# The output projection's first product moved behind the m branch's second half, and the fifth product added to x by VectorE

## The chip, the cores and the metric

The kernel runs on one NeuronCore of one Trainium2 chip. The metric is the device time of one execution in microseconds (us); where several runs were made, the median stands for them. The profile is one execution of the same program, taken by the hardware profiler. TensorE is called PE in its lines, VectorE DVE, ScalarE ACT, GpSimd POOL and SyncE SP; a weight load of TensorE is PEld.

## The reference

The reference is a decoder trunk of two layers on 512 tokens of width 1024 in float32. Each layer has two branches beside each other, joins them, and adds a projection of the sum to `x`; then an MLP follows. The part that matters here is the joining and the output projection:

```
mixed = sigmoid(g_a) * (att @ w_att_branch) + sigmoid(g_m) * (hm @ w_m_branch)
x = x + mixed @ w_out
u = relu(rmsnorm(x, norm_ffn) @ w_ff1)
x = x + (u * u) @ w_ff2
```

`att` and `hm` are 512 x 512, `w_att_branch` and `w_m_branch` 512 x 1024, `w_out` 1024 x 1024. `hm` is the output of the mLSTM branch, here called the m branch.

## The kernel before

**Three matmuls for one.** Float32 operands are split into a high part (rounded to the PE's fast float32 format by an ACT copy) and a low part (what is left, by a DVE subtraction). A product of two split operands takes three PE matmuls (high x high, high x low, low x high), which `mm3` issues. A split (`split`, lines 172 to 181) is one ACT instruction and one DVE instruction that needs its result.

**The m branch's product in two halves.** `m_step(g, m, k)` makes the 512 x 1024 product `hm @ w_m_branch` in two column halves g = 0 and g = 1, with features along the partitions. A half has 16 steps (4 blocks m of 128 columns, 4 blocks k of 128 rows), 48 matmuls in all. When a block m is complete, `merge` reads its PSUM bank on DVE (line 950: gate times product; line 951: added to the attention branch's part in `wide[g]`, the tile `p` of the profile).

**The output projection in seven products.** `mixed @ w_out` is computed by a scheme with seven products in place of eight: tokens, inner columns and output columns are each cut in two, and sums of halves of the operands are multiplied. Each product has 8 steps (4 inner blocks k of 128, 2 token blocks i), 24 matmuls. `p_step(n, k, i)` makes product n. The token operand of each is in `u`, the weight operand in `wo[n, k]`.

- Product 1 multiplies `u[0, 0]`, the first token half of `wide[0]`, which needs only half g = 0 of the m branch.
- Product 5 multiplies `s1`, made by `sum1(p)` from `wide[1]` (line 986), which needs half g = 1. Products 6 and 3 multiply `s2` and `s4`, which `sum_next` makes in place from `s1` (line 992), one from the other. Product 7 multiplies `s3`, made by `sum3` (line 979) from `wide[0]` alone.
- The weight operands are sums of quadrants of `w_out`, built in the tiles `qa` and `qb` by DMAs that add in flight and that POOL issues (`sum_a`, line 1016, and line 1055); each sum may start only when the split of the one before has read the tile. They are split by `ready_w` and `ready_pair`.

**Where results go.** Product 1 fills two PSUM banks called "x", product 5 two called "y", product 2 two called "f". Products 6, 7 and 4 add onto "x", product 3 onto "y". So each product's state of a bank has to be read before the next product writes to it. The table `outs` says how it is read: `onto` lets DVE add (or subtract) the bank to a quarter of `x` (line 1088); `onto_later` lets ACT copy the bank, with its sign, to a staging tile `st` (line 1094), and POOL then adds that to `x` by a DMA (line 1095). The staging tiles are two, taken by i, and share one place for all who stage.

**What sets the order.** The list `fill` gives the steps of PE one after another, each 0.25 wide; the list `side` gives the preparing work (splits, sums, loads, with their places in the same measure), and `weave` merges the two. A scheduler then orders each engine's instructions, with those under `tc.high_priority()` placed ahead. Engines run their own lists in order and wait for each other by semaphores. The places of `side` don't depend on which step of `fill` stands at that place.

Of the kernel before, what the change touches and what calls it, by code (L numbers as in the profile page):

```python
# [33 lines left out]
def hybrid_kernel(ctx, tc, x, norm_mix, w_in, att_q_norm, att_k_norm, att_sinks, m_gate_bias,  # L34
# [50 lines left out]
    def bank():  # L85
        return now["psum"].tile([P, T], F32, tag="m", name=nm("mm"), bufs=5)
# [43 lines left out]
    def g_ffn(l, k):  # L130
        return gcol[:, 16 + 8 * l + k:17 + 8 * l + k]
# [51 lines left out]
    def mm3(ps, sh, sl, mh, ml, first, last, **kw):  # L183
        one = pe.matmul(ps, sh, mh, start=first, stop=False, **kw)
        pe.matmul(ps, sh, ml, start=False, stop=False, **kw)
        pe.matmul(ps, sl, mh, start=False, stop=last, **kw)
        return one
# [201 lines left out]
    def mixer(l, norm, late, order, phase):  # L389
# [303 lines left out]
        def gate_steps(g, last=False):  # L693


            sg = []

            def ev(m, ps):
                sg.append(wide[g][:, m, :] if g < 2 else slot())
                ve.tensor_tensor(sg[m], ps, row[0], op=ALU.mult)  # L700
                if m == 3:
                    for t in sg:
                        i = sc.activation(t, t, AF.Tanh, scale=0.5)  # L703
                    if last:
                        with tc.issue_after(i.ins):
                            sc.preload_act_table_set(LN_EXP)

            return sg, feat_steps(acts, wcols(C_G + 512 * g, 512), ev)
# [147 lines left out]
        g1, s1 = gate_steps(1)  # L856
# [91 lines left out]
        def merge(g, m, ps):  # L948
            t = wide[g][:, m, :]
            ve.scalar_tensor_tensor(sgm[g][m], sgm[g][m], 1.0, ps, op0=ALU.add, op1=ALU.mult)  # L950
            ve.tensor_tensor(t, t, sgm[g][m], op=ALU.add)  # L951
# [16 lines left out]
        def direct(t, g, p):  # L968
            with behind():
                u[t, g, p] = split(part(t, g, p), get=pair)  # L970
# [12 lines left out]
        def sum1(p):  # L983
            if p == 0:
                scratch["b"] = mid.tile([P, 4, H], F32, tag="mid6", name=nm("sc"))
            ve.tensor_tensor(scratch["b"][:, 2 * p:2 * p + 2, :], part(1, 1, p), part(1, 0, p), op=ALU.subtract)
            of_chain("s1", p)
# [79 lines left out]
        def m_step(g, m, k):  # L1067
            if k == 0:
                now_m[g, m] = bank()
            ps, c = now_m[g, m], slice(m * P, (m + 1) * P)  # L1070
            mm3(ps, *(w[:, c] for w in wm[g, k]), *hmT[k], k == 0, k == 3)
            if k == 3:
                with tc.high_priority():
                    merge(g, m, ps)
                    if m % 2:
                        if g:
                            sum1(m // 2)
                        else:
                            direct(0, 0, m // 2)

        now_m = {}
        m_order = [(m, k) for m2, ks in (((0, 1), (0, 1)), ((0, 1), (2, 3))) for m in m2 for k in ks]
# [7 lines left out]
        def onto_later(t, j, i, ps):  # L1090

            with tc.high_priority():
# [1 line left out]
                sc.activation(stage, ps, AF.Copy, scale=-1.0 if j else 1.0)  # L1094
                gp.dma_start(xtok[t][j][:, i, :], stage, accum_op=ALU.add)

        outs = {1: ("x", (0, 0), [(onto_later, 0, 0)]), 5: ("y", "s1", [(onto_later, 1, 1)]),
                6: ("x", "s2", [(onto, 0, 1)]), 3: ("y", "s4", [(onto, 0, 1)]), 7: ("x", "s3", [(onto, 1, 1)]),
                2: ("f", (0, 1), [(onto, 0, 0)]), 4: ("x", (1, 1), [(onto, 1, 0)])}

        def p_step(n, k, i):
            which, key, ends = outs[n]
            fresh = n in (1, 5, 2) and k == 0
            if fresh and i == 0:
                held[which] = [bank(), bank()]
            ah, al = (a[:, k % 2, i * P:(i + 1) * P]
                      for a in u[(*key, k // 2) if isinstance(key, tuple) else (key, k // 2)])
            mm3(held[which][i], ah, al, *wo[n, k], fresh, False, skip_group_check=True)
            if k == 3:
                for f, t, j in ends:  # L1110
                    f(t, j, i, held[which][i])

        def p_steps(n, order_=by_weights):
            return [(0.25, lambda k=k, i=i: p_step(n, k, i)) for k, i in order_]

        norm = Norm(lambda k: g_ffn(l, k))
        fill = [(0.25, lambda m=m, k=k: m_step(0, m, k)) for m, k in m_order] + p_steps(1)
        fill += [(0.25, lambda m=m, k=k: m_step(1, m, k)) for m, k in m_order]
        for n in (5, 6, 3, 7, 2):
            fill += p_steps(n)  # L1120
        fill += p_steps(4, by_tokens)
        side = [(0.3, lambda: ready_w(1, 3)), (2.3, lambda: ready_pair(5, 0)), (4.3, lambda: ready_pair(5, 1)),
# [507 lines left out]
    for l in range(DEPTH):  # L1630
        with start if l == 0 else ExitStack() as phase:
            if l > 0:
                psum_pools(phase, 3)
            norm = mixer(l, norm, late, order, phase)
        late = norm.steps(0, 1.5, 0.5)
        with ExitStack() as phase:
            psum_pools(phase, 2)
            norm = mlp(l, norm, late, phase)
        late = norm.steps(0, 1.5, 0.5, lambda k, norm=norm: turn_behind(norm, k)) if norm else []
        order = [4, 5, 6, 7, 0, 1, 2, 3]  # L1640
# [40 lines left out]
```

## Time and profile before

| | |
|---|---|
| Median of 3 runs | 1286.1 us (1283.01 to 1287.47) |
| The profiled execution's own time | 1284.8 us |
| Its span, first to last instruction | 1283.1 us |
| PE busy | 1267.5 us (99%) |
| PE weight loads busy | 1088.1 us (85%) |
| DVE busy | 1038.5 us (81%) |
| ACT busy | 795.6 us (62%) |
| POOL busy | 260.6 us (20%) |
| Granted PE clock | 1.0 in every slice |

The span is 1.7 us below the execution's own time, and that is 1.3 us below the median of the runs. PE is busy nearly all the time, so what can be gained without taking matmuls away is in the few places where PE waits. The output projection of layer 0 runs from about 260 us to 325 us, that of layer 1 from about 895 us to 960 us. Between and behind them lie the MLPs and the second layer's mixer.

### The profile page before, as it was taken

What the parts mean: (1) busy time and instruction counts of PE and PEld (TensorE: products, weight loads), DVE (VectorE), ACT (ScalarE), POOL (GpSimd) and SP (SyncE); (2) the same over time, 40 slices, a digit from 0 to 9 for tenths busy, and PEclk for the clock granted to TensorE, in tenths of its full rate; (3) what the DMA queues carried; (4) which work ended last, traced back from release to release, by engine and by line L of the source; (5) the groups of instructions that cost most, each with busy time, mean ns of one, the idle gap of its engine ahead of it and who ended that gap; (6) DMA issues with size and microseconds to landing.
All of it is one profiled execution on the core that took longest, in us unless ns stands there. A gap on an engine that the chain in (4) does not pass through costs nothing.

```text
span 1283.1 us, 19225 instructions
## 1 busy us (share of the span) xinstructions
PE 1267.5 (99%) x6882; PEld 1088.1 (85%) x6882; DVE 1038.5 (81%) x1650; ACT 795.6 (62%) x1403; POOL 260.6 (20%) x341
## 2 busy tenths in 40 slices
PE   8999999999999999999999999999999999999998
PEld 6877888887889999999888778888788899999987
DVE  4689988678687897968957889876787879789697
ACT  5478579645665665656554875785465656565563
POOL 4413132021003021131114031310310120301210
PEclk9999999999999999999999999999999999999999
DMA  5426372576669888898224254634856697988953
GB/s 157 111 59 158 106 131 77 154 138 144 186 164 193 234 182 211 195 207 216 34 75 116 63 151 107 115 109 138 164 139 182 164 220 192 201 213 193 212 149 99
DMA packets 139503, 194.39 MB, mean 152 GB/s; under 512 B 10632, under 2 KB 79088, under 8 KB 139408
## 3 DMA queue, kind: packets, MB, share of 16 engines
q1 hardware_dynamic: 92992, 129.72, 33.0%
q0 software_dynamic: 45696, 63.05, 30.7%
q8 instruction: 54, 0.88, 0.3%
q10 hardware_dynamic: 720, 0.40, 0.1%
q14 instruction: 41, 0.34, 0.1%
HBM read 188.95 MB, written 2.10 MB: 149 GB/s over the span
## 4 chain that ended last, share of the span: by engine, by line
PE 86%; DVE 5%; ACT 5%; DMA 2%; issue 1%; DVEq 0%; SPq 0%; ACTq 0%
PE mm L47 70%; PE aux L47 15%; PE aux L52 2%; DMA qa<-in_w_out_dram 1%; ACT t L618 1%; DVE wl L167 1%; DVE p L951 1%; DVE a L950 1%; DMA w<-in_w_in_dram 1%; ACT wh L1162 0%; ACT wh L166 0%; DVE t L653 0%; DVE a L700 0%; ACT t L585 0%; ACT p L703 0%
## 5 line engine op out<-in xcount | busy, mean ns | idle before, releaser
L47 PE MATMUL mm<-i,wh 128*128 128x512 f32 (+1 forms) x1280 | 353.8, 363 | 0.3
L1162 ACT ACTIVATE wh<-raw 128x1024 fp32r<-128x1024 f32 x212 | 223.2, 1056 | 177.6 <-PE mm L47 94.3
L1163 DVE TENSOR_TENSOR wl<-raw,wh 128x1024 fp32r<-128x1024 f32 x212 | 255.6, 1221 | 80.4 <-ACT wh L1162 80.3
L47 PEld LDWEIGHTS mm<-i,wh 128*128 128x128 f32 x1280 | 223.0, 189 | 31.3 <-ACT wh L1162 0.7
L47 PE MATMUL mm<-i,wl 128*128 128x512 f32 (+1 forms) x640 | 229.1, 358 | 0.0
L47 PE MATMUL mm<-wh,uh 128*128 128x512 f32 x440 | 171.8, 390 | 0.0
L47 PE MATMUL mm<-wl,uh 128*128 128x512 f32 x440 | 171.7, 390 | 0.0
L47 PE MATMUL mm<-wh,ul 128*128 128x512 f32 x440 | 171.2, 389 | 0.0
L1332 POOL DMA_DIRECT2D raw<-in_w_ff_dram x48 | 62.5, 1309 | 383.1 <-DMA raw<-in_w_ff_dram 212.9
L47 PEld LDWEIGHTS mm<-i,wl 128*128 128x128 f32 x640 | 120.9, 189 | 18.1
L167 DVE TENSOR_TENSOR wl<-w,wh 128x512 fp32r<-128x512 f32 (+1 forms) x144 | 97.4, 678 | 46.2 <-ACT wh L166 45.1
L166 ACT ACTIVATE wh<-w 128x512 fp32r<-128x512 f32 (+1 forms) x144 | 86.4, 604 | 71.1 <-PE mm L47 49.4
L47 PE MATMUL mm<-wh,i 128*128 128x512 f32 (+1 forms) x352 | 100.6, 359 | 2.2 <-ACT i L179 1.5
L1217 DVE SCALAR_TENSOR_TENSOR x<-mm,ms,x 128x512 f32<-128x512 f32 x126 | 90.6, 744 | 8.5 <-PE mm L47 8.5
L47 PEld LDWEIGHTS mm<-wh,ul 128*128 128x128 f32 x440 | 82.6, 188 | 17.4
L47 PEld LDWEIGHTS mm<-wh,uh 128*128 128x128 f32 x440 | 82.8, 188 | 16.1
L47 PEld LDWEIGHTS mm<-wl,uh 128*128 128x128 f32 x440 | 82.8, 188 | 15.5
L1489 POOL DMA_DIRECT2D raw<-in_w_ff_dram x36 | 43.3, 1204 | 148.4 <-DVE wl L1163 106.1
L47 PEld LDWEIGHTS mm<-wh,i 128*128 128x128 f32 x352 | 62.0, 188 | 12.1 <-ACT i L179 1.9
L47 PE MATMUL aux<-i,wh 128*128 128x256 f32 x384 | 69.6, 283 | 0.0
L47 PE MATMUL aux<-t,wh 128*128 128x256 f32 x384 | 69.6, 283 | 0.0
L47 PE MATMUL mm<-wl,i 128*128 128x512 f32 (+1 forms) x176 | 61.9, 352 | 0.0
(317 smaller groups left out, 2522.0 us busy)
## 6 DMA issues: line engine op xcount, KB each, us to landing
raw<-in_w_ff_dram SPq DMA_DIRECT2D x144, 512.0 KB, 5.1
raw<-in_w_ff_dram POOLq DMA_DIRECT2D x84, 512.0 KB, 7.9
w<-in_w_in_dram SPq DMA_DIRECT2D x112, 256.0 KB, 2.7
a<-in_w_in_dram POOLq DMA_DIRECT2D x32, 256.0 KB, 6.1
qa<-in_w_out_dram POOLq DMA_DIRECT2D x12, 512.0 KB, 6.3
a<-in_w_in_dram SPq DMA_DIRECT2D x16, 256.0 KB, 4.3
w<-in_w_att_branch_dram SPq DMA_DIRECT2D x16, 256.0 KB, 2.9
w<-in_w_m_branch_dram SPq DMA_DIRECT2D x16, 256.0 KB, 2.9
```

Of the source, the lines that this page charges most:

```text
L47: latest[0] = nc.tensor.matmul(*args, **kw)
L52: latest[0] = nc.tensor.transpose(*args)
L166: sc.activation(wh[:, :off], raw[:, :off], AF.Copy)
L167: ve.tensor_tensor(wl[:, :off], raw[:, :off], f32(wh[:, :off]), op=ALU.subtract)
L618: sc.activation(s3[:, i, :], s3[:, i, :], AF.Exp, bias=m[:, i:i + 1], accum_out=den[:, i:i + 1])
L950: ve.scalar_tensor_tensor(sgm[g][m], sgm[g][m], 1.0, ps, op0=ALU.add, op1=ALU.mult)
L951: ve.tensor_tensor(t, t, sgm[g][m], op=ALU.add)
L1162: sc.activation(hi, src, AF.Copy)
L1163: ve.tensor_tensor(lo, src, f32(hi), op=ALU.subtract)
L1217: ve.scalar_tensor_tensor(xh[:, cc], ps[i][:, cc], ms[j][:, b:b + 1], xh[:, cc], op0=ALU.mult, op1=ALU.add)
L1332: gp.dma_start(to[h], src(h, i, j), accum_op=ALU.add)
L1489: gp.dma_start(to[h], src(h, i, j), accum_op=ALU.add)
```

## The change

Product 1 is moved, and the results of product 5 take the other way to `x`. In `fill`, the 8 steps of product 1 stood between the two halves of the m branch's product; now the halves follow each other, and product 1 comes behind the second, ahead of product 5. The places in `side` stay as they are. In `outs`, product 5 gets `onto` in place of `onto_later`. The sign is the same.

```
-        outs = {1: ("x", (0, 0), [(onto_later, 0, 0)]), 5: ("y", "s1", [(onto_later, 1, 1)]),
+        outs = {1: ("x", (0, 0), [(onto_later, 0, 0)]), 5: ("y", "s1", [(onto, 1, 1)]),
...
-        fill = [(0.25, lambda m=m, k=k: m_step(0, m, k)) for m, k in m_order] + p_steps(1)
-        fill += [(0.25, lambda m=m, k=k: m_step(1, m, k)) for m, k in m_order]
-        for n in (5, 6, 3, 7, 2):
+        fill = [(0.25, lambda m=m, k=k: m_step(0, m, k)) for m, k in m_order] + [
+            (0.25, lambda m=m, k=k: m_step(1, m, k)) for m, k in m_order]
+        for n in (1, 5, 6, 3, 7, 2):
```

Both layers get it, since both are built by the same function. What it moves is shown for layer 0; layer 1 moves alike. The rows are the instructions in an engine's order: line, operation, output <- inputs, and the output's size.

On PE, before, at the end of the first half (bank mm_3192 holds its last block m = 3) product 1 follows, into bank mm_3211, with weights wh and wl as first operand:

```order
L47 MATMUL mm_3192<-a_3115,t_2882 128x512
L47 MATMUL mm_3192<-a_3116,t_2882 128x512
L47 MATMUL mm_3192<-a_3115,t_2883 128x512
L47 MATMUL mm_3211<-wh_3040,a_3168 128x512
L47 MATMUL mm_3211<-wl_3041,a_3168 128x512
L47 MATMUL mm_3211<-wh_3040,a_3169 128x512
```

At the same place after the change the second half's first block stands (a_3036 and a_3037 are the split `hm`, a_2691 and a_2692 split weights of the m branch):

```order
L47 MATMUL mm_3192<-a_3115,t_2882 128x512
L47 MATMUL mm_3192<-a_3116,t_2882 128x512
L47 MATMUL mm_3192<-a_3115,t_2883 128x512
L47 MATMUL mm_3211<-a_3036,a_2691 128x512
L47 MATMUL mm_3211<-a_3037,a_2691 128x512
L47 MATMUL mm_3211<-a_3036,a_2692 128x512
```

The 24 matmuls of product 1 now stand behind the 48 of the second half; the 24 of product 5 follow them, and from there PE's list goes on with the same products as before.

On ACT, before, from the splits of `s3` (sc_3234) on. The rows `st` are product 1's two copies (taken from mm_3211 and mm_3212; they stand first) and product 5's; sc_3304 is the tile of s1, s2 and s4, i_3268 the high parts of product 6's weights, t_3291 and t_3335 those of product 3's:

```order
L1094 ACTIVATE st_3261<-mm_3212 128x512
L176 ACTIVATE a_3236<-sc_3234 128x512
L176 ACTIVATE a_3240<-sc_3234 128x512
L176 ACTIVATE i_3268<-qa_2974 128x1024
L176 ACTIVATE t_3291<-t_3222 128x512
L176 ACTIVATE a_3306<-sc_3304 128x512
L176 ACTIVATE i_3268<-qa_2974 128x1024
L176 ACTIVATE t_3335<-t_3227 128x512
L176 ACTIVATE a_3349<-sc_3304 128x512
L176 ACTIVATE a_3366<-sc_3304 128x512
L1094 ACTIVATE st_3403<-mm_3355 128x512
L1094 ACTIVATE st_3418<-mm_3356 128x512
```

After the change, the same stretch (sc_3262 is the tile of s1, s2 and s4; i_3272, t_3295 and t_3336 are the weights; mm_3313 and mm_3314 are product 1's banks):

```order
L176 ACTIVATE a_3236<-sc_3234 128x512
L176 ACTIVATE a_3240<-sc_3234 128x512
L176 ACTIVATE a_3264<-sc_3262 128x512
L176 ACTIVATE i_3272<-qa_2974 128x1024
L176 ACTIVATE t_3295<-t_3221 128x512
L176 ACTIVATE a_3309<-sc_3262 128x512
L176 ACTIVATE i_3272<-qa_2974 128x1024
L1094 ACTIVATE st_3344<-mm_3313 128x512
L1094 ACTIVATE st_3350<-mm_3314 128x512
L176 ACTIVATE t_3336<-t_3227 128x512
L176 ACTIVATE a_3366<-sc_3262 128x512
L176 ACTIVATE a_3370<-sc_3262 128x512
```

Product 1's two copies moved behind the splits of s1 (a_3264 and a_3309), the split of s1's first part moved ahead of product 6's weights, and product 5's copies are gone.

On DVE, before, around the second part of s1 (a_3350 is its low part; a_3125 is the last merge of the second half; the L992 rows turn s1 into s2 and s2 into s4):

```order
L177 TENSOR_TENSOR i_3269<-qa_2974,i_3268 128x1024
L950 SCALAR_TENSOR_TENSOR a_3125<-a_3125,mm_3328 128x512
L177 TENSOR_TENSOR t_3336<-t_3227,t_3335 128x512
L951 TENSOR_TENSOR p_643<-p_643,a_3125 128x512
L986 TENSOR_TENSOR sc_3304<-p_643,p_642 128x512
L177 TENSOR_TENSOR a_3350<-sc_3304,a_3349 128x512
L992 SCALAR_TENSOR_TENSOR sc_3304<-sc_3304,p_642 128x1024
L177 TENSOR_TENSOR a_3367<-sc_3304,a_3366 128x512
L177 TENSOR_TENSOR a_3371<-sc_3304,a_3370 128x512
L177 TENSOR_TENSOR t_3380<-t_3232,t_3379 128x512
L177 TENSOR_TENSOR t_3393<-t_3247,t_3392 128x512
L992 SCALAR_TENSOR_TENSOR sc_3304<-sc_3304,p_643 128x1024
```

After the change, from the second part of s1 on (a_3310 is its low part; mm_3355 and mm_3356 are product 5's banks, x_1_90 the quarter of `x` that it belongs to):

```order
L986 TENSOR_TENSOR sc_3262<-p_643,p_642 128x512
L177 TENSOR_TENSOR t_3296<-t_3221,t_3295 128x512
L177 TENSOR_TENSOR a_3310<-sc_3262,a_3309 128x512
L177 TENSOR_TENSOR i_3273<-qa_2974,i_3272 128x1024
L177 TENSOR_TENSOR t_3337<-t_3227,t_3336 128x512
L992 SCALAR_TENSOR_TENSOR sc_3262<-sc_3262,p_642 128x1024
L177 TENSOR_TENSOR a_3367<-sc_3262,a_3366 128x512
L177 TENSOR_TENSOR a_3371<-sc_3262,a_3370 128x512
L1088 TENSOR_TENSOR x_1_90<-x_1_90,mm_3355 128x512
L1088 TENSOR_TENSOR x_1_90<-x_1_90,mm_3356 128x512
L177 TENSOR_TENSOR t_3380<-t_3232,t_3379 128x512
L177 TENSOR_TENSOR t_3393<-t_3247,t_3392 128x512
```

Product 5's two subtractions now stand between the splits of s2 and product 3's last weights. POOL has two DMAs fewer in each layer, and product 1's two adding DMAs moved behind later weight sums in POOL's list. SP's list keeps its order.

## Prediction

> **What bounds the kernel now.** I read the page's busy shares first, then who PE waits for in the whole run, then PE's timeline over the output projection of each layer, then the chain that led to the wait found there.
>
> ```profile
> PE 1267.5 (99%) x6882; PEld 1088.1 (85%) x6882; DVE 1038.5 (81%) x1650; ACT 795.6 (62%) x1403; POOL 260.6 (20%) x341
> PE mm L47 <- ACT a L176: 3.7, 2, 2.1
> ...
> PE aux L52 <- ACT wh L166: 0.3, 2, 0.2
> ```
>
> PE is the bound. Its longest named wait in the run (us in total, times, longest) is 3.7 us in two places, on a split (line 176): one per layer, both in product 5. The list has nine rows, of which the first and the last stand here; none names lines 1162 or 1163, which split the MLP's weights. PE's timeline (start, duration, instructions, [idle before <- releaser]), layer 0 and then layer 1:
>
> ```profile
> 271.43 0.39 PE L47 MATMUL mm<-wh,a 128*128 128x512 f32 x1
> ...
> 276.89 0.84 PE L47 MATMUL mm<-a,a 128*128 128x512 f32 x3
> ...
> 287.77 2.88 PE L47 MATMUL mm<-i,a 128*128 128x512 f32 x12
> 292.26 8.48 PE L47 MATMUL mm<-i,a 128*128 128x512 f32 x36 [1.61 <-ACT a L176]
> 300.58 5.67 PE L47 MATMUL mm<-t,a 128*128 128x512 f32 x24
> 306.09 0.39 PE L47 MATMUL mm<-wh,a 128*128 128x512 f32 x1
> ```
> ```profile
> 922.38 2.88 PE L47 MATMUL mm<-i,a 128*128 128x512 f32 x12
> 927.40 8.53 PE L47 MATMUL mm<-i,a 128*128 128x512 f32 x36 [2.13 <-ACT a L176]
> 935.76 5.74 PE L47 MATMUL mm<-t,a 128*128 128x512 f32 x24
> 941.34 0.39 PE L47 MATMUL mm<-wh,a 128*128 128x512 f32 x1
> ```
>
> Product 1 starts at 271.43, the second half of the m branch at 276.89, product 5 at 287.77 with 12 matmuls, then PE stands until 292.26; 6 and 3 follow, and product 7 starts at 306.09. The chain of waits says why:
>
> ```profile
> 288.94 0.68 DVE a L950
> 289.62 0.60 DVE t L177
> 290.22 0.61 DVE p L951
> 290.85 0.70 DVE sc L986
> 291.56 0.02 issue
> 291.58 0.64 ACT a L176
> 292.22 0.04 issue
> 292.26 22.16 PE mm L47 x96
> ```
>
> The second part of s1 needs the last merge of the second half, whose matmuls end just before product 5. Only product 5's own first 12 matmuls cover merge, subtraction and split, and DVE comes to the merge 1 us late.
>
> **What the stall is worth.** The second half's 48 matmuls take 287.77 - 276.89 = 10.88 us, 0.2267 us each, so 24 take 5.44 us. From the start of product 5 to that of product 7 are 72 matmuls, 16.32 us. It took 306.09 - 287.77 = 18.32 us in layer 0 and 941.34 - 922.38 = 18.96 us in layer 1: 2.00 and 2.64 us lost, 4.64 together. The idle that is printed is 1.61 + 2.13 = 3.74 us; the rest is the restart and the shorter waits of products 6 and 3 on the same DVE.
>
> **The move of product 1.** It puts 5.44 us of matmuls between the last merge and product 5. I replayed DVE's and ACT's new lists by hand in layer 0's times, with these durations:
>
> ```profile
> L177 DVE TENSOR_TENSOR i<-qa,i 128x1024 fp32r<-128x1024 f32 x3 | 3.7, 1224 | 1.4 <-ACT i L176 1.4
> L951 DVE TENSOR_TENSOR p<-p,a 128x512 f32<-128x512 f32 x6 | 4.1, 688 | 0.1
> L1088 DVE TENSOR_TENSOR x<-x,mm 128x512 f32<-128x512 f32 x2 | 1.4, 682 | 0.6 <-PE mm L47 0.6
> L992 DVE SCALAR_TENSOR_TENSOR sc<-sc,p 128x1024 f32<-128x1024 f32 x2 | 2.4, 1222 | 0.0
> 271.63 0.69 DVE L950 SCALAR_TENSOR_TENSOR a<-a,mm 128x512 f32<-128x512 f32 x1 [0.22 <-PE mm L47]
> ...
> 273.74 0.69 DVE L177 TENSOR_TENSOR a<-p,a 128x512 fp32r<-128x512 f32 x1 [0.70 <-ACT a L176]
> 274.69 1.23 DVE L177 TENSOR_TENSOR i<-qa,i 128x1024 fp32r<-128x1024 f32 x1 [0.26 <-ACT i L176]
> 275.83 1.22 DVE L979 TENSOR_TENSOR sc<-p 128x1024 f32<-128x1024 f32 x1
> 278.24 1.29 DVE L177 TENSOR_TENSOR a<-sc,a 128x512 fp32r<-128x512 f32 x2 [1.18 <-ACT a L176]
> 280.69 1.23 DVE L177 TENSOR_TENSOR i<-qa,i 128x1024 fp32r<-128x1024 f32 x1 [1.16 <-ACT i L176]
> ```
>
> On DVE 128x1024 operations follow each other at 1.14 us (274.69 to 275.83), 128x512 ones at 0.60, or 0.70 where one needs the result of the one before (289.62 to 290.22, 290.85 to 291.56 above); a split's ACT part takes 0.64. The first half ends as before, so the second runs 271.43 to 282.31, product 1 to 287.75, product 5 to 293.2, product 6 to 298.6, product 3 to 304.1, if nothing waits.
>
> - DVE is free at 275.83 and takes the merges as blocks finish (275.7, 277.1, 279.8, 282.5, with 0.2 for the last matmul's way, as in the row at 271.63), with s3 between them. The last merge starts at 282.5; behind it stand a_3265, the add, product 6's first weights (1.14) and then s1's second part, ready at 286.1; ACT's split ends at 286.8, DVE's at 287.5. Product 5 needs them at 287.75 + 2.72 = 290.5: 3.0 us to spare. The first part is ready at 283.7, due at 287.75.
> - s2: i_3273 to 288.9, t_3337 to 290.0 (it waits for ACT, which copies product 1's banks from 287.7 to 288.8), line 992 to 291.2, first split 291.9 and 292.5. Product 6 needs the high part at 293.2 and the low part two matmuls later, 293.65: 1.1 us to spare.
> - s4: the two subtractions of product 5 to 294.3, two weights to 295.5, line 992 to 296.7, split 297.4 and 298.1; due at 298.6 and 299.1: 1.0 us. Its second split follows two adds of product 6, at 300.1, due at 301.8.
>
> So no wait is left up to product 7 in the replay. Bounds: at least the printed 3.74 us if the short waits stay, at most 4.64. I take 4.6, as every margin is 1 us or more, above the shorts' size. Nothing else of PE moves; product 1's operands exist since 274.4 (the row at 273.74), and the five banks in rotation are read by DVE well before they are taken again.
>
> **Product 5's way to x.** Removed per layer: two ACT copies, two adding DMAs; added: two DVE subtractions.
>
> ```profile
> L1094 ACT ACTIVATE st<-mm x8: 580/598/601, 276.4 to 930.5; 128x512 f32<-128x512 f32 x8
> DMA to landing us min/median/max: 3.3/5.5/8.6
> ...
> DMA to landing us min/median/max: 4.5/6.5/8.3
> ...
> 323.93 1.28 DVE L1088 TENSOR_TENSOR x<-x,mm 128x512 f32<-128x512 f32 x2
> ```
>
> The landing times are those of line 1095 (to x) and of line 1055 (product 7's weight sums). ACT gains 2 x 0.60 us and waits anyway: zero. DVE pays 2 x 0.60, inside the 5.44 us of product 6; in the s4 sum above, cost zero on PE. Were that cover gone, 1.2 us a layer. DVE now waits for PE at these two, and t_3380, t_3393, s4 and its splits are queued behind. Product 1's two copies sit in front of s2's split on ACT, but that one waits for DVE until 291.2: zero. They are also done (288.8) before product 6 adds onto the same banks (293.2).
>
> The pages were read against this too. "Perfetto Trace Analysis" of the Trainium skill, section "Optimizing Scalar/DVE Operations", gives VectorE about 125 ns of access overhead on PSUM against 60 on SBUF, and ACT 51 against 93, which speaks for leaving the bank to ACT; by that the four subtractions would cost 4 x 0.065 = 0.26 us more of DVE. The trace doesn't show it: 682 ns with a PSUM input, 688 without.
>
> **Queues.** POOL: product 1's second adding DMA now stands behind a weight sum that needs i_3273 (288.9) and one that needs t_3337 (290.0), so it is issued at about 291 in place of 278 and lands by 300 with the longest landing shown (8.6). That quarter of x is next read by product 2's add, in the row at 323.93: hidden. The first three of product 7's weight sums are issued up to 12 us ahead of it, the last at 296.7; with 8.3 us to land it is there at 305, needed at 307. SP keeps its order; its loads of product 2's weights wait for PE's use of m branch tiles, which ends 5.5 us earlier, and the MLP's second load waits for product 1's staging, free before product 5's was: earlier, worth nothing to PE.
>
> **What comes behind.** PE's waits name no line of the MLP's weights, so layer 0's gain should pass through the MLP into layer 1.
>
> **Rivals.**
>
> 1. The stall moves to product 6 or 3. For: the same DVE work stays due, and margins are 1.0 to 1.1 us; against: DVE had waits to fill between 271 and 281 (0.70, 0.26, 1.18, 1.16 us in the rows above). If DVE is 3.3 us later than replayed, each layer pays 2.2 us again: 4.6 - 4.4 = 0.2 us gained, 1285.9; 2.2 us later gives 4.6 - 2.2 = 2.4, 1283.7.
>
> 2. Slower, by a late weight sum. DMA is full where the chain needs the second part of product 6's weights:
>
> ```profile
> 278.00:285.00 7.00, 7.00 (x32) 5.81 (x31) 5.54 (x8) 2.30 (x4) 3.39 (x4) 1.00 1.01 163
> 276.21 1.21 POOL L1016 DMA_DIRECT2D qa<-in_w_out_dram  x1 [3.91 <-DVE i L177]
> 286.46 1.04 ACT L176 ACTIVATE i<-qa 128x1024 fp32r<-128x1024 f32 x1
> 287.02 0.53 SPq L1189 DMA_DIRECT2D raw<-in_w_ff_dram  x1
> DMA to landing us min/median/max: 5.7/6.3/9.0
> ```
>
> The stretch's DMA share (second last column) is 1.01. The MLP's first 512 KB load now goes at about 282.5, when s3's split has freed its place, in place of 287.0. ACT reaches this weight at 286.7, in order, and s2 stands behind it. The landing times are those of line 1016. From landing to s2's first split 5.3 us pass (1.05 + 1.2 + 0.6 on ACT, 0.6 + 1.2 on DVE, 0.64 on ACT), so it must land by 287.9; the longest landing, 9.0 from 277.4, is 286.4. It decides beyond 287.9 + 2.3 = 290.2, 12.8 us after issue; at 15 us each layer pays 4.5 us, 9.0 - 4.6 = 4.4 us slower, 1290.5. Against it: product 1's 2 x 256 KB leave that stretch. "DMA: Bandwidth & Descriptors" of the Trainium skill, section "Anatomy of one DMA — SWDGE (gpsimd) path", fits 2.0 us + bytes / 436e3 to such a DMA, by which 512 KB would take an estimated 3.2 us and never be late. The rows, 5.7 to 9.0 us, are above it, and the rival goes by them.
>
> 3. One layer's gain is lost behind the projection, because loads pace the MLP: 1286.1 - 2.64 = 1283.5. For: PE's idle is only named, not the slack behind it; against: the absent waits.
>
> **How the numbers follow.** From its own 1284.8 us the execution comes to 1280.2; the median of the runs stands 1.3 us above it, so I forecast 1286.1 - 4.6 = 1281.5 us. A measurement of this kernel tells about 0.3%, 3.9 us. Chances: forecast 0.62, rival 1 0.18, rival 3 0.10, rival 2 0.10. The forecast is a gain of 0.29% to 0.36%, so 0.06 of it counts as within 0.3%, with rivals 1 and 3: faster 0.56, same 0.34, slower 0.10. Range: 1279.2 (4.64 us from the median and half the runs' spread, 2.2) to 1286.0 (rival 1); rival 2 and some of each tail are left out.
>
> **What would show it.** Right: PE's wait on line 176 in product 5 gone in both layers; 16.3 us from product 5's start to product 7's; the m branch's 96 matmuls without a gap; ACT's `st` rows four, at about 288 and 920 (634.6 us later, less layer 0's gain). Wrong: a PE wait at product 6 or 3 on a split of line 176 or 177 (rivals 1, 2; with ACT waiting for `qa` before it, rival 2), or first waits of PE inside an MLP (rival 3).

## The result and the profile after

The changed kernel takes 1278.74 us, the median of 6 runs (1278.26 to 1278.96). The kernel before took 1283.04 us beside it (6 runs, 1282.71 to 1287.47). The medians lie 4.3 us apart. The ratio is 0.9962, with a 95% interval of 0.9951 to 0.9972: faster by 0.38% (4.9 us by this ratio), a little more than the 0.3% that a measurement can tell from no change. In a later comparison it was 1278.54 against 1283.29 us, 4.75 us apart, ratio 0.9962 (0.9948 to 0.9976). The forecast of 1281.5 us is 2.8 us too high, and the time lies 0.46 us below the low end of its range.

The profiled execution took 1278.87 us, with a span of 1277.2 us. Its page's busy shares:

```profile
PE 1267.0 (99%) x6882; PEld 1089.3 (85%) x6882; DVE 1040.0 (81%) x1654; ACT 793.5 (62%) x1399; POOL 257.0 (20%) x337
```

From the list of PE's waits in the whole run (us in total, times, longest), the first and the last of seven rows:

```profile
PE aux L52 <- DVE t L653: 1.8, 4, 0.5
...
PE aux L47 <- ACT t L585: 0.2, 1, 0.2
```

The row that led this list before, 3.7 us on a split of line 176, is gone. PE's timeline over the same place, layer 0 and then layer 1:

```profile
287.35 11.04 PE L47 MATMUL mm<-i,a 128*128 128x512 f32 x48
298.23 5.60 PE L47 MATMUL mm<-t,a 128*128 128x512 f32 x24
303.67 0.39 PE L47 MATMUL mm<-wh,a 128*128 128x512 f32 x1
...
919.56 11.04 PE L47 MATMUL mm<-i,a 128*128 128x512 f32 x48
930.44 5.60 PE L47 MATMUL mm<-t,a 128*128 128x512 f32 x24
935.88 0.39 PE L47 MATMUL mm<-wh,a 128*128 128x512 f32 x1
```

Products 5 and 6 are one row of 48 matmuls without idle time, and product 3 follows. From product 5's start to product 7's are 303.67 - 287.35 = 16.32 us, and 935.88 - 919.56 = 16.32 us: PE's own time for 72 matmuls, to the hundredth. Before, it was 18.32 and 18.96 us.

DVE's timeline in layer 0, from the second part of s1 to the split of s4:

```profile
285.05 0.68 DVE L986 TENSOR_TENSOR sc<-p,p 128x512 f32<-128x512 f32 x1
...
289.49 1.22 DVE L992 SCALAR_TENSOR_TENSOR sc<-sc,p 128x1024 f32<-128x1024 f32 x1
291.40 1.29 DVE L177 TENSOR_TENSOR a<-sc,a 128x512 fp32r<-128x512 f32 x2 [0.70 <-ACT a L176]
292.61 1.28 DVE L1088 TENSOR_TENSOR x<-x,mm 128x512 f32<-128x512 f32 x2
...
295.02 1.22 DVE L992 SCALAR_TENSOR_TENSOR sc<-sc,p 128x1024 f32<-128x1024 f32 x1
```

s2's first high part is there at about 291.4, when DVE may begin its half of the split; product 6 begins at 287.35 + 5.44 = 292.8. So 1.4 us are to spare there. Product 5's two subtractions (line 1088) stand where the prediction put them.

A second place is shorter too, the start of the MLP. Before, PE's first matmul of the MLP in layer 0 (the row mm<-i,wh) came 325.35 - 306.09 = 19.26 us after product 7's start:

```profile
324.29 0.92 PE L52 MATMUL aux<-ident,x 128*128 128x128 f32 x6
325.35 0.70 PE L47 MATMUL mm<-i,wh 128*128 128x512 f32 x2
```

Now it comes 322.54 - 303.67 = 18.87 us after it:

```profile
321.86 0.93 PE L52 MATMUL aux<-ident,x 128*128 128x128 f32 x6
322.54 0.71 PE L47 MATMUL mm<-i,wh 128*128 128x512 f32 x2
```

In layer 1 it is 19.25 us before and 18.88 us now, so the two layers gain 0.77 us here. What went is a wait of PE's weight load (PEld) for ACT's split of an MLP weight (line 1162). The two pages have it in the row of these loads, in the last column (idle time before them, and what ended most of it). Before:

```profile
L47 PEld LDWEIGHTS mm<-i,wh 128*128 128x128 f32 x1280 | 223.0, 189 | 31.3 <-ACT wh L1162 0.7
```

Now:

```profile
L47 PEld LDWEIGHTS mm<-i,wh 128*128 128x128 f32 x1280 | 223.0, 189 | 30.4
```

### The profile page after: what moved, and what is told of

It is laid out like the page before. It is cut to its first block, busy times and chain, and to the rows that moved or that the text cites. A ratio compares the mean times of both kernels' runs of the same rounds, so it can differ in the third digit from the quotient of the medians.

```text
span 1277.2 us, 19227 instructions
## 1 busy us (share of the span) xinstructions
PE 1267.0 (99%) x6882; PEld 1089.3 (85%) x6882; DVE 1040.0 (81%) x1654; ACT 793.5 (62%) x1399; POOL 257.0 (20%) x337
## 4 chain that ended last, share of the span: by engine, by line
PE 92%; ACT 3%; DVE 3%; issue 1%; DMA 1%; DVEq 0%; SPq 0%
PE mm L47 75%; PE aux L47 15%; PE aux L52 2%; DVE wl L167 1%; ACT t L618 1%; DMA w<-in_w_in_dram 0%; ACT wh L166 0%; ACT t L585 0%; DVE t L653 0%; ACT p L703 0%; DVE t L586 0%; DMA x<-in_x_dram 0%; ACT L703 0%; ACT t L649 0%; ACT kT L563 0%
## 5 line engine op out<-in xcount | busy, mean ns | idle before, releaser
L47 PEld LDWEIGHTS mm<-i,wl 128*128 128x128 f32 x640 | 120.9, 189 | 18.1
```

Of the source, the lines that this page charges most:

```text
L47: latest[0] = nc.tensor.matmul(*args, **kw)
```

## The experiments

**The kernel before, profiled again.** Nothing is changed.

> The kernel before, unchanged, profiled a second time. What it tells apart: whether the first profile of before (span 1283.1 us, 18.32 and 18.96 us from product 5's start to product 7's) was a usual execution. The theory that only the level was off expects a span of about 1281.3 us (the four lower runs of before are 1282.7 to 1283.1 us, and the time is 1.7 us above the span), with about 2.0 us lost in each layer's products 5 to 3, so that the change is worth 4.0 us there. The theory that the first profile was usual expects a span of 1283 us and again 2.0 and 2.6 us.

It took 1284.04 us, with a span of 1282.3 us, between the two that I had named. PE's rows at the start of product 5 and of product 7, layer 0 and layer 1:

```profile
287.39 2.88 PE L47 MATMUL mm<-i,a 128*128 128x512 f32 x12
...
305.95 0.39 PE L47 MATMUL mm<-wh,a 128*128 128x512 f32 x1
...
922.47 2.88 PE L47 MATMUL mm<-i,a 128*128 128x512 f32 x12
...
940.59 0.39 PE L47 MATMUL mm<-wh,a 128*128 128x512 f32 x1
```

They are 18.56 and 18.12 us apart, so 2.24 and 1.80 us were lost, 4.04 together, where the first profile lost 4.64. The waits in product 5 were 1.74 and 1.34 us in place of 1.61 and 2.13. The chain of waits says what moves them. In the first profile of before, it passes through these two transfers, one per layer (start, and duration from issue to landing):

```profile
271.10 8.47 DMA qa<-in_w_out_dram
...
905.68 9.04 DMA qa<-in_w_out_dram
```

In the second profile of before:

```profile
270.69 8.64 DMA qa<-in_w_out_dram
...
905.75 8.26 DMA qa<-in_w_out_dram
```

These are adding DMAs of line 1016, half of a weight sum for product 6. ACT splits that sum as soon as it lands, DVE makes the low part, and the merges stand behind this work on DVE. The transfer's duration less PE's wait is 8.47 - 1.61 = 6.86, 9.04 - 2.13 = 6.91, 8.64 - 1.74 = 6.90 and 8.26 - 1.34 = 6.92 us. So in these four layers PE's wait is the duration of one DMA less 6.9 us.

**The move alone.** Product 5 still goes by ACT's copies and adding DMAs.

```
-        fill = [(0.25, lambda m=m, k=k: m_step(0, m, k)) for m, k in m_order] + p_steps(1)
-        fill += [(0.25, lambda m=m, k=k: m_step(1, m, k)) for m, k in m_order]
-        for n in (5, 6, 3, 7, 2):
+        fill = [(0.25, lambda m=m, k=k: m_step(0, m, k)) for m, k in m_order] + [
+            (0.25, lambda m=m, k=k: m_step(1, m, k)) for m, k in m_order]
+        for n in (1, 5, 6, 3, 7, 2):
```

> Product 1 is moved, product 5's results still go over ACT's copies and POOL's adding DMAs. If the move's cover alone is what counts and product 5's way to x is free on PE, this equals the changed kernel (-4.3 us against before). My own account expects a new wait: the two staging tiles are still in flight from product 1 (adding DMA issued at 288 and 291 us, 3.3 to 8.6 us to land) when ACT wants to fill them with product 5's banks at about 293, and s4's split stands behind the second copy on ACT. Landing at 297 gives product 3 a wait of about 0.5 us in each layer, landing at 300 one of 3 us: -4.3 + 1 = -3.3 us, at worst +1.5 us against before.

It took 1286.70 us (10 runs, 1285.5 to 1288.14) against 1283.43: ratio 1.0021 (1.0010 to 1.0032), 3.3 us slower than before by the medians. PE's timeline, layer 0 and layer 1:

```profile
286.98 11.04 PE L47 MATMUL mm<-i,a 128*128 128x512 f32 x48
300.72 7.33 PE L47 MATMUL mm<-t,a 128*128 128x512 f32 x24 [2.70 <-ACT a L176]
...
937.45 7.63 PE L47 MATMUL mm<-t,a 128*128 128x512 f32 x24 [2.46 <-ACT a L176]
```

The wait in product 5 is gone, and a longer one stands ahead of product 3. ACT's timeline in layer 0 shows why:

```profile
293.51 0.60 ACT L1094 ACTIVATE st<-mm 128x512 f32<-128x512 f32 x1 [1.47 <-DMA x<-st]
...
299.56 0.60 ACT L1094 ACTIVATE st<-mm 128x512 f32<-128x512 f32 x1 [4.92 <-DMA x<-st]
300.05 1.14 ACT L176 ACTIVATE a<-sc 128x512 fp32r<-128x512 f32 x2
```

Product 5's copies need the staging tiles that product 1's adding DMAs still read. Before, product 1 staged some 10 us earlier; now it stages just ahead. ACT stands 4.92 us for the second tile, and s4's split is queued behind. In the chain of waits that DMA stands as 8.88 us from 290.57 on.

The wait is not all of the loss. The same 24 matmuls took 5.60 us in the changed kernel, and 7.33 and 7.63 here. The windows of PE (start:end, length, busy, granted clock, DMA share, GB/s):

```profile
300.72:304.50 3.78, 3.78 (x10) 0.55 0.81 145
304.50:307.90 3.40, 3.40 (x17) 1.00 0.61 176
```

For 3.8 us behind the wait PE's clock was granted at 0.55, which costs 0.45 x 3.8 = 1.7 us on top of the wait. My own account had the wait, up to 3 us a layer, but not this cost, and its worst case was 1.5 us slower. The profiled execution, at 1287.95 us, is one of four from 1287.95 to 1288.14 with a mean granted clock of 0.997 over the run; the other six, from 1285.5 to 1286.79, have 0.998 or 0.999.

**The other way to x alone.** Product 1 stays in its old place.

```
-        outs = {1: ("x", (0, 0), [(onto_later, 0, 0)]), 5: ("y", "s1", [(onto_later, 1, 1)]),
+        outs = {1: ("x", (0, 0), [(onto_later, 0, 0)]), 5: ("y", "s1", [(onto, 1, 1)]),
```

> Product 1 stays between the halves, product 5's results are subtracted by DVE. If DVE's two subtractions were free on PE here too, the time is that of before. My account: without the cover of product 1 DVE is the late engine, and 1.2 us more of it stand ahead of s4; product 3 then waits for s4's split about 0.8 us in each layer: about 1.6 us slower than before, with the 1.6 to 2.1 us wait in product 5 unchanged.

It took 1283.23 us (10 runs), ratio 0.9999 (0.9990 to 1.0009). My 1.6 us were a miss: no wait appeared at product 3. DVE took the two subtractions in gaps in which it waited for ACT, and ACT, without its copies, split s2's two parts one behind the other. The wait in product 5 stayed, 1.33 and 1.61 us (1.79 and 2.06 us lost from product 5's start to product 7's), and it again follows from the two transfers in the chain (8.22 - 1.33 = 6.89, 8.51 - 1.61 = 6.90):

```profile
270.62 8.22 DMA qa<-in_w_out_dram
...
905.10 8.51 DMA qa<-in_w_out_dram
```

**The move with staging tiles of its own for product 5.** If the shared tiles are the cause of the new wait, giving product 5 two others must remove it.

```
-                stage = mid.tile([P, T], F32, tag=("sel", "cm2")[i], name=nm("st"))
+                stage = now["tmp"].tile([P, T], F32, tag="t", name=nm("st")) if j else mid.tile(
+                    [P, T], F32, tag=("sel", "cm2")[i], name=nm("st"))
```

> Product 1 moved and product 5 still copied by ScalarE and added by DMAs, as in the run with the move alone, but with staging tiles of its own for product 5 (two of the pool of 18 temporary tiles), so that its copies need not wait for product 1's adding DMAs. Theory (the new wait at product 3 there is ScalarE queued behind a copy that waits for the staging tile): the waits of 2.70 and 2.46 us at product 3 go, products 5 to 3 run unbroken, and the time is the changed kernel's within 0.5 us, 1278.3 to 1279.2. Rival (the copies themselves, or the order in which ScalarE takes them, make the split late): a wait of 0.6 to 1.2 us a layer stays at product 3, some 1281 to 1282.5 us. Rival (the adding DMAs slow what else runs): no wait and yet over 1280.

It took 1279.12 us (5 runs, 1278.56 to 1279.19), ratio 0.9962 (0.9949 to 0.9975); the changed kernel beside it took 1278.54 us. PE's timeline in layer 0:

```profile
287.07 11.04 PE L47 MATMUL mm<-i,a 128*128 128x512 f32 x48
297.95 5.60 PE L47 MATMUL mm<-t,a 128*128 128x512 f32 x24
```

ACT's timeline there:

```profile
292.57 1.06 ACT L1095 ACTIVATE st<-mm 128x512 f32<-128x512 f32 x2
294.80 1.16 ACT L176 ACTIVATE a<-sc 128x512 fp32r<-128x512 f32 x2 [1.17 <-DVE sc L992]
```

The copies wait for no DMA, s4's split is early, and nothing is left of the wait. From product 5's start to product 7's are 16.32 us in both layers, as in the changed kernel. So what the second half of the change does for PE is only to free the staging tiles; the copies and the adding DMAs cost PE nothing in this stretch.

**Product 6's weights later.** The kernel before, with two entries of `side` moved behind the second half of the m branch, so that the merges no longer stand behind them.

```
-                (4.9, sum3), (6.2, lambda: ready_pair(6, 0)), (8.6, lambda: ready_pair(6, 1)),
+                (4.9, sum3), (6.2, lambda: ready_pair(6, 0)), (10.1, lambda: ready_pair(6, 1)),
...
-        side += [(at, lambda k=k: ready_w(3, k)) for k, at in enumerate((7.3, 9.3, 10.7, 11.2))]
+        side += [(at, lambda k=k: ready_w(3, k)) for k, at in enumerate((7.3, 10.2, 10.7, 11.2))]
```

> The kernel before, with two preparing steps put later in the list (the second part of product 6's weights and the second block of product 3's), so that DVE takes the last merge of the m branch's second half at once. Product 1 stays between the halves. If the wait in product 5 comes only from the two splits in front of the merge, the wait goes (about 0.3 us left of 1.6) and the kernel gains 3 us or more. If what is missing is time on DVE up to product 6, the wait moves: about 0.3 us in product 5 and 1.5 us at product 6 for s2's first split, 18.1 us from product 5's start to product 7's in place of 18.3, and the time stays that of before within 0.5 us.

It took 1284.26 us (10 runs, 1283.89 to 1284.95), ratio 1.0004 (0.9995 to 1.0013). The wait goes to product 6; PE, layer 0:

```profile
290.77 3.04 PE L47 MATMUL mm<-i,a 128*128 128x512 f32 x12 [0.18 <-ACT a L176]
295.38 5.73 PE L47 MATMUL mm<-i,a 128*128 128x512 f32 x24 [1.57 <-ACT a L176]
```

From product 5's start to product 7's are 18.68 us in both layers, not the 18.1 expected. So this order of DVE's work doesn't help: its work up to product 6 has to fit beside matmuls, and these were missing. But the chain of this wait no longer passes through the DMA (it goes from PE's matmuls to the last merge), and the runs span only 1.06 us, where those of before span over 5 beside them (1281.94 to 1287.32).

**Half of product 1 moved.** The lines that these replace in the changed kernel are left out.

```
+        first = p_steps(1)
+        fill = [(0.25, lambda m=m, k=k: m_step(0, m, k)) for m, k in m_order] + first[:4]
+        fill += [(0.25, lambda m=m, k=k: m_step(1, m, k)) for m, k in m_order] + first[4:]
+        for n in (5, 6, 3, 7, 2):
```

> First four steps of product 1 between the halves of m, last four behind them; product 5 by onto. Theory (the products behind the halves are cover, 0.2267 us a matmul): the cover that is missing in the kernel before, 1.3 to 2.6 us a layer, shrinks by the 2.7 us of 12 matmuls moved, so at most some 0.5 us a layer of waiting is left at product 6 (its split's margin in the changed kernel is 1.15 to 1.4 us with 24 matmuls of cover, and 24 less 12 leaves it 1.3 to 1.6 us short by that measure). Two estimates therefore: about 1279.3 us (0.5 us a layer late) or, if the margin is taken as measured, 1281.4 us (1.4 us a layer). Rival (the order alone counts, any product behind the halves is enough): same as the changed kernel, 1278.7.

It took 1279.76 us (9 runs, 1278.86 to 1280.45) against 1283.03, ratio 0.9973 (0.9963 to 0.9983). Of the two estimates the first, 1279.3 us, is near, but not by its mechanism: no wait comes at product 6. DVE's timeline:

```profile
286.81 1.22 DVE L177 TENSOR_TENSOR i<-qa,i 128x1024 fp32r<-128x1024 f32 x1
287.94 0.69 DVE L986 TENSOR_TENSOR sc<-p,p 128x512 f32<-128x512 f32 x1
...
290.54 1.22 DVE L992 SCALAR_TENSOR_TENSOR sc<-sc,p 128x1024 f32<-128x1024 f32 x1
```

s1's second part is 2.9 us later than in the changed kernel (287.94 against 285.05), but s2 only 1.05 (290.54 against 289.49): the scheduler did product 6's weights ahead of s1, while DVE would have waited for PE. I had shifted DVE's list as a block. So 12 matmuls of cover are enough for all but 0.1 us a layer: from product 5's start to product 7's are 16.42 us (16.32 in the changed kernel). This kernel is still 0.77 us above the next one, which ran on the same chip and has 16.45 us there. The start of the MLP is the difference: from product 7's start to it are 19.26 and 19.25 us here, as before the change, and 18.88 and 18.87 us in the next one. All fourteen profiles agree: PE's weight load waits there for ACT's split of an MLP weight, 0.7 us in the two layers, in each of the seven kernels or executions that have some of product 1 between the halves, and in none of the seven that have all of it behind them. Why the place of product 1 decides this, the views don't show.

**Product 1 by DVE too.** The changed kernel without any staging.

```
-        outs = {1: ("x", (0, 0), [(onto_later, 0, 0)]), 5: ("y", "s1", [(onto, 1, 1)]),
+        outs = {1: ("x", (0, 0), [(onto, 0, 0)]), 5: ("y", "s1", [(onto, 1, 1)]),
```

> The changed kernel with product 1's results too taken up by VectorE out of PSUM: two more 128x512 operations on VectorE (2 x 0.61 = 1.2 us) about 287.5 us into the run, no copies by ScalarE and no adding transfers there. Theory (VectorE's time up to product 6's second operand is what is short, with 1.15 us to spare in the changed kernel): the margin is used up, TensorE waits 0 to 0.3 us a layer at product 6, so 1278.5 to 1279.5 us. Rival (VectorE's work at this place is free as long as a product is behind the halves): 1278.7 with no wait. Rival (the adding transfers slow others): faster by some 0.5 us or more.

It took 1278.99 us (6 runs, 1278.57 to 1279.56), ratio 0.9969 (0.9958 to 0.9981): as the changed kernel, with no wait at product 6 and 0.13 us a layer lost at product 3 (16.45 us from product 5's start to product 7's). DVE took the two adds at 286.44 and did s2 at 289.37, where the changed kernel did it at 289.49, since without ACT's copies its two waits of 0.26 us for ACT fell away.

**More work on DVE.** Two kernels test the margin: the changed one with two and with six 128x1024 operations ahead of s2 (once and three times the pair).

```
+                if key == "s2":
+                    for _ in range(1):
+                        ve.tensor_tensor(b, b, wide[g][:, :, 0:H], op=ALU.add)
+                        ve.tensor_tensor(b, b, wide[g][:, :, 0:H], op=ALU.subtract)
```

> The changed kernel with two extra 128x1024 operations on VectorE ahead of product 6's second operand (an array added to a tile and taken away again; the results are the same up to rounding), some 2 x 1.14 = 2.3 us. Theory (margin of 1.15 us a layer): TensorE waits 1.1 to 1.3 us a layer ahead of product 6, about 2.4 us in all, so 1281.1 us. Rival (the splits are paced by something else, the weight loads or ScalarE): no wait, 1278.7.

> The changed kernel with six such operations, 6.8 us a layer. Theory: past the margin each us costs a us, 6.8 - 1.15 = 5.7 us a layer, 1290.1 us, the wait in the stretch of products 6 and 3. Between this run and the one with two, 4.6 us a layer more, 9.1 us in all. Rival: less, if product 3 and the products after it take back some of it by work that VectorE does later.

They took 1282.23 us (10 runs, 1281.86 to 1282.56) and 1297.07 us (4 runs, 1296.36 to 1297.79). With two operations, PE in layer 0:

```profile
287.26 5.60 PE L47 MATMUL mm<-i,a 128*128 128x512 f32 x24
293.86 5.97 PE L47 MATMUL mm<-i,a 128*128 128x512 f32 x24 [0.99 <-ACT a L176]
```

DVE's two operations and s2 are 2.5 us later relative to PE; with 1.4 us to spare, product 6 has to be 1.1 us late, and starts at 293.86 in place of 287.26 + 5.44 = 292.70. So far that is as forecast, but the time is 1.1 us above the forecast 1281.1. Another 0.37 us a layer were lost within product 6 (5.97 us in place of 5.60): here DVE did product 5's two subtractions (at 293.06) ahead of the low part of s2 (at 294.25). With six, PE's timeline in layer 0:

```profile
299.83 7.06 PE L47 MATMUL mm<-i,a 128*128 128x512 f32 x24 [7.10 <-ACT a L176]
```

The windows of PE behind that wait:

```profile
299.83:303.60 3.77, 3.77 (x11) 0.63 0.49 144
303.60:306.73 3.13, 3.13 (x16) 1.00 0.93 146
```

I had forecast 5.7 us a layer; from product 5's start to product 7's 8.7 and 9.1 us were lost. The operations took 1.25 us each, not 1.14, since each needs the one before; product 5's subtractions went between them (1.2 us); and behind the wait the clock was 0.63 for 3.8 us, another 1.4 us. A long wait costs more than its length.

**The kernel before with s1 a little later.** The chain's length is changed in small steps: the second subtraction of s1 is done two times, and three times.

```
-            ve.tensor_tensor(scratch["b"][:, 2 * p:2 * p + 2, :], part(1, 1, p), part(1, 0, p), op=ALU.subtract)
+            for _ in range(2 if p else 1):
+                ve.tensor_tensor(scratch["b"][:, 2 * p:2 * p + 2, :], part(1, 1, p), part(1, 0, p), op=ALU.subtract)
```

> The kernel before with one VectorE operation more ahead of product 5's second operand: the second subtraction of the first chain sum (128x512) is done twice, with the same result, some 0.61 to 0.69 us. TensorE's waits of 1.3 to 2.1 us a layer there become about 1.9 to 2.8 us. Theory (a wait of TensorE from about 2.4 us on lowers the granted clock behind it: after waits of 2.46 and 2.70 us it was 0.78 and 0.55, after 1.61 and 2.13 us it was 1.00): where a wait stays under it, the layer costs 0.65 us more, where it goes over it, 1.7 to 1.9 us on top, so single runs fall into groups at about 1284.5, 1286.3 and 1288, and a median between 1284.5 and 1287. Rival (each us of waiting costs a us): 1283.2 + 2 x 0.65 = 1284.5, with the spread of before.

> The same with the subtraction done three times, 1.2 to 1.35 us more; the waits become 2.5 to 3.4 us. Theory (clock): both layers go over the bound, 1283.2 + 2 x 1.3 + 2 x 1.5 to 1.9 = 1288.8 to 1289.6 us, with a granted clock under 0.85 in the 7 us after each wait. Rival (each us costs a us): 1285.8 us, clock 1.00.

Done twice, it took 1287.02 us against 1284.02, ratio 1.0022 (1.0012 to 1.0032): at the upper end of the theory's 1284.5 to 1287, and above the rival's 1284.5. The mean granted clock of each run is on record and sorts the 12 runs into the three groups: three from 1284.16 to 1285.49 with 0.999 or 1.000, five from 1286.22 to 1287.63 with 0.998, four from 1288.95 to 1289.78 with 0.997. The profiled execution is the fastest of them. The two transfers in its chain:

```profile
270.48 7.83 DMA qa<-in_w_out_dram
...
905.27 8.20 DMA qa<-in_w_out_dram
```

Its PE timeline, layer 0 and layer 1:

```profile
291.73 8.53 PE L47 MATMUL mm<-i,a 128*128 128x512 f32 x36 [1.69 <-ACT a L176]
...
926.89 8.48 PE L47 MATMUL mm<-i,a 128*128 128x512 f32 x36 [2.06 <-ACT a L176]
```

Duration less wait is now 6.14 us in both layers, 0.76 less than 6.9, about what one more operation takes (0.70). The transfers happened to be short, so the waits stayed at what they were before. Done three times, it took 1289.34 us (5 runs, 1287.19 to 1290.01), ratio 1.0035 (1.0022 to 1.0048). PE's timeline in layer 0:

```profile
292.40 10.08 PE L47 MATMUL mm<-i,a 128*128 128x512 f32 x36 [3.23 <-ACT a L176]
```

The window of PE behind that wait:

```profile
292.40:296.20 3.80, 3.79 (x10) 0.57 0.66 112
```

The clock falls to 0.57 for 3.8 us behind the wait. The transfer in this chain took 8.65 us, and 8.65 - 3.23 = 5.42 is another 0.72 less. The median lies in the theory's 1288.8 to 1289.6 us, and no run is as low as the rival's 1285.8; but two of the five, 1287.19 and 1287.42 us, are under the theory's range, with a mean clock of 0.999 and 0.998 where the others have 0.997.

**The changed kernel again.**

> The changed kernel unchanged, to see how firm its level is. As before within its runs so far: 1278.3 to 1279.0 us, ratio 0.996 to 0.997, no wait of TensorE in products 5, 6 and 3. Rival (its level varies from execution to execution as that of the kernel before does): runs spread over 2 us and more.

It took 1278.54 us (5 runs, 1278.12 to 1278.95). All eleven runs of the changed kernel lie within 0.84 us. Of the 77 runs of the kernel before that were made beside others, 16 lie above 1285 us, and the median of the 77 is 1283.3. The share differs between comparisons, from 1 of 20 to 6 of 17.

## Why the prediction was right or wrong

**What the stall is worth: right for the execution that was read, and near the whole gain partly by luck.** 16.32 us from product 5 to product 7 in both layers mean that the stall is all gone, and in the profile that was read it was worth 4.64 us. That was a large one: before, profiled again, lost 4.04 us there, and the kernel with product 5 by DVE alone 3.85. The measured gain, 4.3 to 4.75 us by the medians, is a stall below 4.64 and the 0.77 us at the start of the MLPs, which the prediction did not count.

**Where the stall comes from: incomplete.** The prediction read the chain from 288.94 on and saw DVE come to the last merge 1 us late. Followed 18 us further back, the chain passes through the transfer of a weight sum (271.10 to 279.57 in layer 0). The wait is that transfer's duration less 6.9 us, in six layers of three profiles (the two of before, and the one with product 5 by DVE alone), and so it is no constant of the kernel.

**The move: right.** The replay of DVE's and ACT's lists agrees with the trace to about 0.4 us, s2's margin by its high part was 1.4 us where the replay had 293.2 - 291.9 = 1.3, and the extra operations on DVE found the margin where the trace has it. The half move shows the limit of such a replay: it cannot see that the scheduler will fill DVE's waits in another way.

**Product 5's way to x: zero alone, but not beside the move.** Taken as a term, "cost zero on PE" held: alone it changes nothing. What the prediction did not name is what this edit is for. It listed the shared staging tiles only for the MLP's load, and never asked what product 5's copies would wait for if they stayed. Without this edit the move is 3.3 us slower than before, with a wait at product 3 as rival 1 has it, but behind a staging tile and not behind DVE. The edits don't add up: 3.3 us slower and no change apart, 4.3 us faster together.

**Queues: right; what comes behind: a term put at nothing.** Product 1's second adding DMA was issued at 290.95 (forecast about 291), the MLP's first load went at 282.08 (282.5), and PE has no wait up to product 7. "PE's waits name no line of the MLP's weights" is true of PE's own list; the row of PE's weight loads on the same page names line 1162, 0.7 us in the two layers. The profiled execution gained 1.3 us beyond the forecast 1280.2. Of this, 0.77 us are that wait, and 0.4 us lie before the m branch of layer 0, ahead of the change's place: the m branch starts anywhere from 258.8 to 260.3 us in the fourteen profiles.

**Rivals: none came.** In the changed kernel no wait went to product 6 or 3, no weight sum was late, and layer 1 got its gain.

**The level: the step that failed.** "The median of the runs stands 1.3 us above it, so I forecast 1286.1 - 4.6 = 1281.5 us." Two of the three runs behind that median, 1286.1 and 1287.47, belong to the 16 of 77 that lie above 1285. The kernel's usual time is 1283.3 (1283.04 beside the result), so the level was about 3 us too high, and that is the forecast's 2.8 us. 1283.3 - 4.6 = 1278.7 is what was measured; that it fits so closely is luck, since the 4.6 was too large for the stall and left out the MLPs. Taking 1.3 us for a constant offset that passes to the changed kernel was probably wrong in kind too: the runs above 1285 seem to come from the stall itself and to go with it, since the eleven runs of the changed kernel, which has no stall, lie within 0.84 us. The range's low end, the median less 4.64 and half the spread, inherited the error.

For the origin of the runs above 1285 us the evidence is indirect. PE's clock stayed at 1.00 behind waits of up to 2.13 us and fell behind waits of 2.46 us and more, at 1.4 to 1.7 us each in the windows above. With transfers of 8.3 to 9.0 us before's waits are 1.3 to 2.1 us, under that bound; by these figures a few tenths to one microsecond more in the transfer would bring a layer over it, at some 1.7 us besides. The runs' mean clocks fit: of the 71 runs of before that have one on record, the 44 at 1.000 took 1281.94 to 1284.98 us and the 8 at 0.998 took 1285.38 to 1287.32, with the 19 at 0.999 on both sides (1283.05 to 1286.8). So at least part of the runs above 1285 had a lower clock somewhere; that it was behind this wait is not shown. The kernel with s1 later by one operation fell into three groups of runs, as no layer, one or two over the bound would give. The kernel with the DMA out of the chain has no run above 1285 among ten, which is weak by itself: at 16 of 77 ten runs without one would come by chance about one time in ten. An execution of before above 1285 us was not itself profiled.

## What to carry to other kernels

Follow the chain of a wait back to the transfer or the engine that starts it, and compare two profiles there: if a landing time sets the wait, the wait varies, and three runs don't give a level. When independent work is moved next to a producer that stages its results, look at who shares the staging tiles, and price the combination rather than each edit. Putting off VectorE's work only moved the wait; 12 matmuls of cover between the producer and the engine that waits for it removed all but 0.1 us of it. Read the waits of PE's weight loads beside those of its matmuls: 0.7 us stood in them alone.

## What the runs showed of the hardware

In these runs a wait of TensorE cost more than itself from somewhere between 2.13 and 2.46 us on. Behind 0.99, 1.33, 1.61, 1.74 and 2.13 us the granted clock was 1.00; behind 2.70, 3.23 and 7.10 us (layer 0 of three kernels) it was 0.55, 0.57 and 0.63 for some 3.8 us, and about full after that: 1.4 to 1.7 us lost. Behind 2.46 us (layer 1 with the move alone) it was 0.77 over the 7.46 us of product 3, which is again 1.7 us, not all of it at once. "TensorE: Matmul & The Clock Gate" of the Trainium skill, section "What's actually happening", describes the clock gate and puts the idle window that lowers the clock at about 3.4 us and lets it run free of the program; the 3.8 us at the lower clock are near that figure, but here a wait of 2.46 us was already enough, and the measurement decides.

An adding DMA holds its source tile long: in the kernel with the move alone line 1095's transfer of 256 KB took 8.88 us from issue to landing, and the next copy into that tile waited for it, against 0.60 us for the copy that fills its tile.
